# One of three weight sums of a seven-product pair moved from VectorE to an accumulating DMA

## The chip, the cores and the metric

The kernel runs on one core of a Trainium2 chip. A core has TensorE (PE: matmuls; PEld is its weight load, which overlaps them), VectorE (DVE), ScalarE (ACT), GpSimd (POOL) and SyncE (SP). Each of the five works through its own queue in order; semaphores order them against each other. SP, ACT and POOL can issue DMAs, which run on the core's 16 DMA engines. The metric is the device time of one execution in microseconds, as the median of several runs. The profile is one more execution, taken by the hardware profiler.

## The reference

A decoder trunk of two layers on 256 tokens of width 2048, in float32, beside 256 memory tokens. Only the matrix products matter here:

```python
mem_n = _rmsnorm(mem, norm_mem)
for layer in range(DEPTH):                                   # 2: HGRN2, then GLA
    hn = _rmsnorm(h, norm_mix[layer])
    y, xq = mixer(hn, w_in)                                  # gated linear recurrence on one input projection
    xa = _memory_attention(xq, mem_n, w_mem_kv[layer])
    h = h + jnp.concatenate([y, xa], axis=-1) @ w_out[layer]
    hn = _rmsnorm(h, norm_ffn[layer])
    gate, up = jnp.split(hn @ w_gate_up[layer], 2, axis=-1)  # 2048 -> 2 x 5632
    h = h + (jax.nn.silu(gate) * up) @ w_down[layer]         # 5632 -> 2048
return _rmsnorm(h, norm_final)
```

Every weight is read from HBM once, some 430 MB in all, and the 256 tokens make two tiles of 128.

## The kernel before, in words

**Products in parts.** A float32 operand is split in two parts of the narrower type `float32r`: the high part is a cast on ACT, the low part is what the cast left over, a subtraction on DVE (`split`, lines 276 to 291). A product of two operands is then three matmuls: high by high, high by low, low by high. Each has 128 rows and up to 512 columns.

**Pairs.** Weights come in tiles `raw` of 128 partitions by 4 blocks of 512 columns (1 MB, three buffers). Such a tile holds a *pair*: two row blocks (k = 0, 1) of the weight by two column blocks that begin at `c0` and `c1`. Against the two token tiles that is a 2 x 2 by 2 x 2 block product, which would take eight products. A pair of kind "S" takes seven, in the way of Strassen and Winograd, with sums of blocks on both sides (`seven`, lines 420 to 434): four blocks of a side and three sums that build on each other give seven factors. Kinds "O", "H" and "-" take eight products with fewer sums or none. An S pair costs 21 matmuls instead of 24. In return DVE has the sums of the weights to make, and seven blocks to split instead of four.

**An S pair's work before the change**, in the order in which DVE takes it: split of block 0 (one block, "a"), split of blocks 2 and 3 ("b"), then three sum instructions, in place in `raw` (one of two blocks at once, two of one block), then the splits of the sums, blocks 0 and 1 ("c") and blocks 2 and 3 ("d"). Each split is preceded by its cast on ACT. When "d" is done, the buffer is free, and SP can issue the loads of the pair three further on (`load_pair`, lines 408 to 418: two DMAs of 512 KB, first both row blocks of `c0`, then both of `c1`; the load's tile and the pair's parts wait for each other by semaphores that the framework sets). The split parts lie in six buffers `parts`, so DVE can run about two pairs ahead of PE.

**Sums on the other side.** The activations' factors are made once for each pair by `Forms.put` (feed-forward), `further` (mixers, output, memory), with the same three sums, on small tiles of 128 x 128.

**Where S pairs stand.** `project_two` (memory keys and values, mixers' input projections, the output projection, the last down projections) takes pairs by a plan such as "----SSS-". `project_halves` runs the gate/up projection: for each of 11 blocks of 512 columns eight pairs by a string of `KINDS`, "SSOSSOSS" for the last seven blocks of a layer; between two such blocks stand two down projections of an earlier part, with plain splits and no sums (`weights`, 4 tiles a block).

**What sets the order.** In the feed-forward, PE, DVE and ACT keep the program's order (`Engine.kept`); elsewhere the framework's scheduler orders each engine's queue by the program's order and readiness. Side work (decays, scores, readouts, transposes of the mixers) is cut in pieces and put between pairs (`later`, `step`). POOL does little: powers for the norms (`rstd`, line 189), memsets such as that of the scores `sc` (line 912), and one low part in each feed-forward block, which waits for a sum on DVE (`free_port`, line 286). No DMA is issued by POOL before the change.

Most operations are recorded at line 151, the wrapper that issues them; they are told apart by tiles: `raw<-raw` are the sums of weights, `parts<-raw` the splits, `f_p` the gate/up products, `fd` the down products, `hf`, `hv` those of HGRN, `gk`, `gg` of GLA, `wo` of the output, `m0p`, `m1p` of the memory.

Of the kernel before, what the change touches and what calls it, by code (L numbers as in the profile page):

```python
# [9 lines left out]
F32 = mybir.dt.float32  # L10
# [3 lines left out]
AF = mybir.ActivationFunctionType  # L14
ALU = mybir.AluOpType
AX = mybir.AxisListType

P = 128
# [22 lines left out]
def trunk_kernel(ctx: ExitStack, tc: tile.TileContext, x, mem, norm_mix, norm_ffn, norm_mem,  # L41
                 norm_final, hgrn_w_in, hgrn_lb_logits, hgrn_onorm, gla_w_in, gla_w_gk,
                 gla_b_gk, gla_onorm, w_mem_kv, w_out, w_gate_up, w_down, c_ident, c_mask, out):
    nc = tc.nc
# [117 lines left out]
    pe, ve, ac = Engine(nc.tensor), Engine(nc.vector), Engine(nc.scalar)  # L162
# [110 lines left out]
        n_w[0] += 1  # L273
        return i, wts.tile([P, 4, 512], F32, tag="raw", name=f"raw{i}", bufs=3)

    def split(src, name, by=2):

        n, m = src.shape[1:]
        if n == 1:
            both = wts.tile([P, 2, 1, 512], F32R, tag="part", name=f"parts{name}", bufs=2)  # L280
        else:
            both = wts.tile([P, 2, 2, 512], F32R, tag="parts", name=f"parts{name}", bufs=6)
        for k in range(0, n, by):
            j = min(k + by, n)
            ac.copy(out=both[:, 0, k:j, 0:m], in_=src[:, k:j, :])
            low = (nc.gpsimd if free_port else ve).tensor_tensor(  # L286
                out=both[:, 1, k:j, 0:m], in0=src[:, k:j, :], in1=both[:, 0, k:j, 0:m].bitcast(F32), op=ALU.subtract)
            if free_port:
                tc.add_manual_dep(low.ins, free_port.pop(), mybir.DependencyInfo(
                    mybir.DependencyClass.Sync, mybir.DependencyReason.DATA), reason="port")  # L290
        return [(both[:, 0, k, 0:m], both[:, 1, k, 0:m]) for k in range(n)]
# [67 lines left out]
    class Forms:  # L359
# [20 lines left out]
        def put(self, ps, gains):  # L380

            g = work.tile([P, 8, P], F32, tag="stg", name=f"{self.name}g", bufs=2)
            for k in range(2):
                ac.activation(out=g[:, 2 * k:2 * k + 2, :], in_=ps[:, 2 * k * P:(2 * k + 2) * P].rearrange(
                    "p (a t) -> p a t", t=P), func=AF.Copy, scale=gains[k])
            tt = ve.tensor_tensor

            def parts(i, j, n):
                ac.copy(out=self.h[:, i:i + n, :], in_=g[:, j:j + n, :])
                tt(out=self.l[:, i:i + n, :], in0=g[:, j:j + n, :], in1=self.h[:, i:i + n, :].bitcast(F32), op=ALU.subtract)  # L390

            if self.kind == "O":
                tt(out=g[:, 4:6, :], in0=g[:, 1:3, :], in1=g[:, 0:4:3, :], op=ALU.subtract)
                parts(0, 0, 6)
                return
            ve.scalar_tensor_tensor(out=g[:, 4, :], in0=g[:, 0, :], scalar=-1.0, in1=g[:, 3, :],
                                           op0=ALU.mult, op1=ALU.subtract)
            tt(out=g[:, 5, :], in0=g[:, 1, :], in1=g[:, 0, :], op=ALU.subtract)
            tt(out=g[:, 6, :], in0=g[:, 3, :], in1=g[:, 5, :], op=ALU.subtract)
            tt(out=g[:, 7, :], in0=g[:, 2, :], in1=g[:, 6, :], op=ALU.subtract)  # L400
            parts(0, 0, 8)
            if self.kind == "B":
                tt(out=g[:, 4, :], in0=g[:, 2, :], in1=g[:, 3, :], op=ALU.subtract)
                parts(8, 4, 1)

    TIMES = {"S": (1,) * 7, "O": (0, 2, 2, 2, 2, 0, 0), "H": (0, 2, 2, 2, 1, 0, 1)}

    def load_pair(raw, w, p, c0, c1, n):

        if n_w[0] == 1:  # L410
            for k, j, c in ((0, 0, c0), (0, 1, c1), (1, 3, c0), (1, 2, c1)):
                nc.sync.dma_start(out=raw[:, j, 0:n], in_=w[(2 * p + k) * P:(2 * p + k + 1) * P, c:c + n])
                if k == 0 and c == c1:
                    load_mem(0, 256, 512)
            return
        for j, c in ((slice(0, 4, 3), c0), (slice(1, 3), c1)):
            nc.sync.dma_start(out=raw[:, j, 0:n],
                              in_=w[2 * p * P:(2 * p + 2) * P, c:c + n].rearrange("(k p) c -> p k c", p=P))

    def seven(i, raw, between=None):  # L420

        n = raw.shape[2]
        tt = ve.tensor_tensor
        b00, = split(raw[:, 0:1, :], f"{i}a")
        b11, b10 = split(raw[:, 2:4, :], f"{i}b")
        if between:
            between()

        tt(out=raw[:, 0:2, :], in0=raw[:, 0:4:2, :], in1=raw[:, 1:2, :].broadcast_to([P, 2, n]), op=ALU.subtract)
        tt(out=raw[:, 2, :], in0=raw[:, 2, :], in1=raw[:, 0, :], op=ALU.add)  # L430
        tt(out=raw[:, 3, :], in0=raw[:, 3, :], in1=raw[:, 2, :], op=ALU.subtract)
        t5, t7 = split(raw[:, 0:2, :], f"{i}c")
        t6, t4 = split(raw[:, 2:4, :], f"{i}d")
        return {1: ("x00", b00), 2: ("x01", b10), 3: ("z", b11), 4: ("x11", t4), 5: ("s", t5), 6: ("u", t6), 7: ("d0", t7)}

    def further(g):

        tt = ve.tensor_tensor
        ve.scalar_tensor_tensor(out=g[:, 4, :], in0=g[:, 1, :], scalar=-1.0, in1=g[:, 3, :], op0=ALU.mult, op1=ALU.subtract)
        tt(out=g[:, 5, :], in0=g[:, 0, :], in1=g[:, 1, :], op=ALU.subtract)  # L440
        tt(out=g[:, 6, :], in0=g[:, 3, :], in1=g[:, 5, :], op=ALU.subtract)
        tt(out=g[:, 7, :], in0=g[:, 2, :], in1=g[:, 6, :], op=ALU.subtract)

    class Pair:

# [70 lines left out]
    def project_two(pairs, plan, w, c0, c1, n, name, give, view=lambda ps: ps, onto=None, prep=None, behind=None,  # L516
# [7 lines left out]
        ps, out = {}, []  # L524
# [35 lines left out]
        for at, (p, kind) in enumerate(zip(order, plan)):  # L560
            i, raw = new_raw()
            if i == 0:
                load_pair(raw, w, p, c0, c1, n)
            if prep:
                prep(at)
            if i > 0:
                load_pair(raw, w, p, c0, c1, n)
            if kind == "S":
                todo = held(behind, seven, i, raw[:, :, 0:n]) if behind else seven(i, raw[:, :, 0:n])
                last = at == plan.rindex("S")  # L570
                for b in (1, 6, 7, 5, 2, 4, 3) if last else (3, 2, 1, 5, 7, 6, 4):
                    product(b, pairs[p].get(todo[b][0]), todo[b][1])
                if last and at == len(plan) - 1:
                    early()
                elif len(pending) > MANY:
                    step()
                continue
            b00, b01 = split(raw[:, 0:2, 0:n], f"{i}a", 2 if i else 1)
            b11, b10 = split(raw[:, 2:4, 0:n], f"{i}b")
            if at > 0 and at == plan.rindex("S") + 1:  # L580
                early()
            for k, (lf, rt) in enumerate(((b00, b01), (b10, b11))):
                step()
                for b, t, right_factor in ((2, 0, lf), (4, 1, lf), (8, 1, rt), (3, 0, rt)):
                    if b == 8 and len(pending) > MANY:
                        step()
                    product(b, pairs[p].x(k, t), right_factor)
# [3 lines left out]
    def project_halves(forms, kinds, w, c0, c1, name, key, keep):  # L591
# [15 lines left out]
        for p, kind in enumerate(kinds):  # L607
            Engine.kept = keep <= p
            i, raw = new_raw()
            load_pair(raw, w, p, c0, c1, 512)  # L610
            x = forms[p].get
            last = p == len(PAIRS) - 1
            if kind == "S":
                todo = seven(i, raw, lambda: mark(key + p))
                for b in (1, 2, 6, 7, 5, 4, 3) if last else (1, 3, 2, 5, 7, 6, 4):
                    product(b, x(todo[b][0]), todo[b][1])
            else:
                b00, b01 = split(raw[:, 0:2, :], f"{i}a")
                mark(key + p)
                b11, b10 = split(raw[:, 2:4, :], f"{i}b")  # L620
                todo = [[(2, "x00", b00), (5, "x10", b01), (4, "x10", b00), (3, "d0", b01)]]
                if kind == "O":
                    todo.append([(2, "x01", b10), (5, "x11", b11), (4, "x11", b10), (3, "d1", b11)])
                else:
                    ve.tensor_tensor(out=raw[:, 3, :], in0=raw[:, 3, :], in1=raw[:, 2, :], op=ALU.subtract)
                    e1, = split(raw[:, 3:4, :], f"{i}c")
                    todo.append([(2, "x01", b10), (3, "x01", b11), (7, "x11", b11), (4, "x11", e1)])
                todo = [m for ms in zip(*todo) for m in ms] if last else todo[0] + todo[1]
                for b, f, right in todo:
                    product(b, x(f), right)  # L630
            step()
# [639 lines left out]
    scale = lambda ss=ss: h_scale(ss, "rx", True)  # L1271
    for l in range(2):
# [6 lines left out]
        turned = []  # L1279
# [26 lines left out]
        if l == 0:  # L1306
            hq = {}
            ffn(0, hq2, r2, lambda n: h_quad(hq, n, g_mix[1], ss, "hm1_", sevens=2))
            scale = lambda ss=ss: h_scale(ss, "rm1", True)
# [79 lines left out]
```

## Time and profile before

| | before |
|---|---|
| median of 3 runs | 2270.07 us (2270.04 to 2271.07) |
| the profiled execution's own time | 2271.69 us |
| its span | 2269.9 us |
| PE busy | 2250.8 us, 99% |
| DVE busy | 2065.8 us, 91% |
| ACT busy | 1423.5 us, 63% |
| POOL busy | 83.4 us, 4% |
| granted TensorE clock | 0.999 |
| read from HBM | 430.71 MB |

How to read it: busy time is the union of an engine's instructions. A group of instructions is written as line, engine, operation, out<-in, shapes, count, then busy us and mean ns of one, then the engine's idle time just before them and what ended it. The row of a wait names who waited, for whom, and the total, number and longest of the waits. In the chain, each piece has its start, its length and what it was. Windows count from the span's start.

### The profile page before, as it was taken

Reading aid. Unit: us, or ns where it says so; the run is one execution under the profiler, and the core shown is the slowest. Engines: PE = TensorE matmul, PEld = TensorE weight load, DVE = VectorE, ACT = ScalarE, POOL = GpSimd, SP = SyncE. Lnnn points to the kernel's source line nnn. Section 1 sums busy time; section 2 is a strip of 40 time slices with the busy share of each in tenths; the row PEclk is TensorE's granted clock in tenths of the full one; section 3 lists DMA queues with packets and bytes.
Section 4 is the critical chain, followed back from the end, with each engine's and each line's share of the span. In section 5 each row is a group of like instructions: output and inputs, shape, how many; then the busy total and the mean of one; then the engine's idle time right before and its main releaser. Section 6 shows DMA issues by size and latency. Waiting matters only on the chain.

```text
span 2269.9 us, 29374 instructions
## 1 busy us (share of the span) xinstructions
PE 2250.8 (99%) x10710; PEld 1901.4 (84%) x10710; DVE 2065.8 (91%) x2615; ACT 1423.5 (63%) x1938; POOL 83.4 (4%) x61
## 2 busy tenths in 40 slices
PE   9999999999999999999999999999999999999998
PEld 7888888888888888888889999988888888888887
DVE  7889999899999999999996887899899999999997
ACT  6655656566666666666665665566566666666664
POOL 0000000000000000000000000001000000000000
PEclk9999999999999999999999999999999999999999
DMA  8645545455556665555665446555556565665564
GB/s 289 204 151 183 186 157 177 167 168 203 170 202 222 204 206 190 203 199 204 204 212 174 142 146 190 157 176 203 197 194 203 205 210 194 205 205 202 205 217 153
DMA packets 232644, 435.78 MB, mean 192 GB/s; under 512 B 13199, under 2 KB 42675, under 8 KB 232243
## 3 DMA queue, kind: packets, MB, share of 16 engines
q1 hardware_dynamic: 231203, 429.64, 56.4%
q10 hardware_dynamic: 1296, 4.26, 0.5%
q8 instruction: 84, 1.38, 0.2%
q14 instruction: 61, 0.50, 0.1%
HBM read 430.71 MB, written 3.15 MB: 191 GB/s over the span
## 4 chain that ended last, share of the span: by engine, by line
PE 89%; DVE 6%; ACT 2%; issue 1%; DMA 1%; POOL 0%; SPq 0%; POOLq 0%; DVEq 0%; ACTq 0%
PE f_p L151 39%; PE fd L151 19%; PE wo L151 4%; PE m1p L151 2%; PE wo0p L151 2%; PE hf0p L151 2%; PE wo1p L151 2%; PE fd_0p L151 2%; PE gk1p L151 1%; PE gg11p L151 1%; PE gg10p L151 1%; PE gg01p L151 1%; PE m0p L151 1%; DVE raw L151 1%; PE gx L151 1%
## 5 line engine op out<-in xcount | busy, mean ns | idle before, releaser
L151 DVE TENSOR_TENSOR raw<-raw 128x512 f32<-128x512 f32 (+3 forms) x474 | 403.6, 852 | 9.2
L151 ACT CAST parts<-raw 128x1024 fp32r<-128x1024 f32 (+1 forms) x216 | 212.0, 1016 | 44.6 <-DMA raw<-in_w_down_dram 9.8
L151 DVE TENSOR_TENSOR parts<-raw,parts 128x1024 fp32r<-128x1024 f32 (+1 forms) x196 | 224.0, 1180 | 15.2 <-ACT parts L151 15.1
L286 POOL TENSOR_TENSOR parts<-raw,parts 128x1024 fp32r<-128x1024 f32 x20 | 48.2, 2411 | 1187.1 <-ACT parts L151 1138.6
L151 ACT COPY h<-fd 128x512 f32<-128x512 f32 x80 | 46.3, 588 | 55.0 <-PE fd L151 52.1
L151 ACT ACTIVATE s<-s,rf_r 128x512 f32<-128x512 f32 x44 | 31.8, 722 | 41.6 <-DVE s L151 41.4
L151 DVE TENSOR_TENSOR e<-f_p,e 128x512 f32<-128x512 f32 x66 | 45.2, 685 | 2.3
L151 ACT COPY fd<-h 128x512 f32<-128x512 f32 x82 | 45.2, 582 | 0.0
L151 PE MATMUL fd<-parts,s_6h 128*128 128x512 f32 x128 | 39.8, 392 | 0.0
L151 PE MATMUL fd<-parts,s_8h 128*128 128x512 f32 x128 | 39.8, 392 | 0.0
L151 PE MATMUL fd<-parts,s_4h 128*128 128x512 f32 x128 | 39.8, 392 | 0.0
L151 PE MATMUL fd<-parts,s_2h 128*128 128x512 f32 x128 | 39.8, 392 | 0.0
L151 PE MATMUL fd<-parts,s_0h 128*128 128x512 f32 x128 | 39.8, 392 | 0.0
L151 PE MATMUL fd<-parts,s_5h 128*128 128x512 f32 x128 | 39.4, 389 | 0.0
L151 PE MATMUL fd<-parts,s_3h 128*128 128x512 f32 x128 | 39.4, 389 | 0.0
L151 PE MATMUL fd<-parts,s_7h 128*128 128x512 f32 x128 | 39.4, 389 | 0.0
L151 PE MATMUL fd<-parts,s_1h 128*128 128x512 f32 x128 | 39.4, 389 | 0.0
L151 DVE TENSOR_TENSOR s<-f_p,e 128x512 f32<-128x512 f32 x44 | 30.3, 689 | 4.3 <-PE f_p L151 2.4
L151 DVE SCALAR_TENSOR_TENSOR s<-e,rf_r,s 128x512 f32<-128x512 f32 x44 | 31.0, 747 | 0.2
L151 PEld LDWEIGHTS fd<-parts,s_7h 128*128 128x128 f32 x128 | 24.0, 188 | 5.0
L151 PEld LDWEIGHTS fd<-parts,s_3h 128*128 128x128 f32 x128 | 24.0, 188 | 5.0
L151 PEld LDWEIGHTS fd<-parts,s_1h 128*128 128x128 f32 x128 | 24.0, 188 | 5.0
(5723 smaller groups left out, 7258.1 us busy)
## 6 DMA issues: line engine op xcount, KB each, us to landing
raw<-in_w_gate_up_dram SPq DMA_DIRECT2D x352, 512.0 KB, 3.9
raw<-in_w_down_dram SPq DMA_DIRECT2D x80, 1024.0 KB, 5.7
raw<-in_hgrn_w_in_dram SPq DMA_DIRECT2D x96, 512.0 KB, 3.9
raw<-in_gla_w_in_dram SPq DMA_DIRECT2D x96, 384.0 KB, 3.3
raw<-in_w_out_dram SPq DMA_DIRECT2D x16, 1024.0 KB, 5.8
raw<-in_w_out_dram SPq DMA_DIRECT2D x32, 512.0 KB, 4.1
raw<-in_w_mem_kv_dram SPq DMA_DIRECT2D x30, 512.0 KB, 5.5
raw<-in_w_down_dram SPq DMA_DIRECT2D x16, 512.0 KB, 4.1
```

The costliest lines, as they stand in the source:

```text
L151: ins = func(*args, **kwargs)
L286: low = (nc.gpsimd if free_port else ve).tensor_tensor(out=both[:, 1, k:j, 0:m], in0=src[:, k:j, :], in1=both[:, 0, k:j, 0:m].bitcast(F32) ...
```

## The change

Signs of the seven products are chosen anew, so that the first weight sum is a plain sum of two blocks as they lie in HBM, block 1 (k = 0, `c1`) plus block 2 (k = 1, `c1`). `load_pair` loads the `c1` half first, and for an S pair POOL then issues a DMA of 256 KB that adds block 2 from HBM onto block 1 in `raw`. It has to wait for the `c1` load, and the first sum on DVE has to wait for it. DVE keeps two sums: one of one block, which uses the added block, and one of two blocks. The split of blocks 0 and 1 is taken with the opposite sign (`turned`): ACT casts with scale -1, DVE makes the low part with a scalar_tensor_tensor. Before, that split gave the factors of products 5 and 7, now of 6 and 7, and the order of products follows. The sums of the activations change sign accordingly; in `Forms.put` two of them become one instruction.

```diff
-    def split(src, name, by=2):
+    def split(src, name, by=2, turned=False):
...
+            if turned:
+                hi = both[:, 0, k:j, 0:m]
+                ac.activation(out=hi, in_=src[:, k:j, :], func=AF.Copy, scale=-1.0)
+                ve.scalar_tensor_tensor(out=both[:, 1, k:j, 0:m], in0=src[:, k:j, :], scalar=-1.0, in1=hi.bitcast(F32),
+                                        op0=ALU.mult, op1=ALU.subtract)
+                continue
...
# Forms.put
-            ve.scalar_tensor_tensor(out=g[:, 4, :], in0=g[:, 0, :], scalar=-1.0, in1=g[:, 3, :],
-                                           op0=ALU.mult, op1=ALU.subtract)
-            tt(out=g[:, 5, :], in0=g[:, 1, :], in1=g[:, 0, :], op=ALU.subtract)
-            tt(out=g[:, 6, :], in0=g[:, 3, :], in1=g[:, 5, :], op=ALU.subtract)
-            tt(out=g[:, 7, :], in0=g[:, 2, :], in1=g[:, 6, :], op=ALU.subtract)
+            tt(out=g[:, 4:6, :], in0=g[:, 3:0:-2, :], in1=g[:, 0:1, :].broadcast_to([P, 2, P]), op=ALU.subtract)
+            ve.scalar_tensor_tensor(out=g[:, 6, :], in0=g[:, 3, :], scalar=-1.0, in1=g[:, 5, :],
+                                    op0=ALU.mult, op1=ALU.subtract)
+            tt(out=g[:, 7, :], in0=g[:, 2, :], in1=g[:, 6, :], op=ALU.add)
...
-    def load_pair(raw, w, p, c0, c1, n):
+    def load_pair(raw, w, p, c0, c1, n, kind):
...
-        for j, c in ((slice(0, 4, 3), c0), (slice(1, 3), c1)):
+        for j, c in ((slice(1, 3), c1), (slice(0, 4, 3), c0)):
             nc.sync.dma_start(out=raw[:, j, 0:n],
                               in_=w[2 * p * P:(2 * p + 2) * P, c:c + n].rearrange("(k p) c -> p k c", p=P))
+        if kind == "S":
+            nc.gpsimd.dma_start(out=raw[:, 1, 0:n], in_=w[(2 * p + 1) * P:(2 * p + 2) * P, c1:c1 + n], accum_op=ALU.add)
...
# seven
-        tt(out=raw[:, 0:2, :], in0=raw[:, 0:4:2, :], in1=raw[:, 1:2, :].broadcast_to([P, 2, n]), op=ALU.subtract)
-        tt(out=raw[:, 2, :], in0=raw[:, 2, :], in1=raw[:, 0, :], op=ALU.add)
-        tt(out=raw[:, 3, :], in0=raw[:, 3, :], in1=raw[:, 2, :], op=ALU.subtract)
-        t5, t7 = split(raw[:, 0:2, :], f"{i}c")
-        t6, t4 = split(raw[:, 2:4, :], f"{i}d")
+        tt(out=raw[:, 0, :], in0=raw[:, 1, :], in1=raw[:, 0, :], op=ALU.subtract)
+        tt(out=raw[:, 2:4, :], in0=raw[:, 2:4, :], in1=raw[:, 0:1, :].broadcast_to([P, 2, n]), op=ALU.subtract)
+        t6, t7 = split(raw[:, 0:2, :], f"{i}c", turned=True)
+        t5, t4 = split(raw[:, 2:4, :], f"{i}d")
...
# project_two, and the like in project_halves
-                for b in (1, 6, 7, 5, 2, 4, 3) if last else (3, 2, 1, 5, 7, 6, 4):
+                for b in (1, 6, 7, 5, 2, 4, 3) if last else (3, 2, 1, 6, 7, 5, 4):
```

More of the change, by code (lines that the diff above doesn't have):

```diff
@@ L438, in further @@
         tt = ve.tensor_tensor
-        ve.scalar_tensor_tensor(out=g[:, 4, :], in0=g[:, 1, :], scalar=-1.0, in1=g[:, 3, :], op0=ALU.mult, op1=ALU.subtract)
+        tt(out=g[:, 4, :], in0=g[:, 3, :], in1=g[:, 1, :], op=ALU.subtract)
         tt(out=g[:, 5, :], in0=g[:, 0, :], in1=g[:, 1, :], op=ALU.subtract)
-        tt(out=g[:, 6, :], in0=g[:, 3, :], in1=g[:, 5, :], op=ALU.subtract)
-        tt(out=g[:, 7, :], in0=g[:, 2, :], in1=g[:, 6, :], op=ALU.subtract)
+        ve.scalar_tensor_tensor(out=g[:, 6, :], in0=g[:, 3, :], scalar=-1.0, in1=g[:, 5, :], op0=ALU.mult, op1=ALU.subtract)
+        tt(out=g[:, 7, :], in0=g[:, 2, :], in1=g[:, 6, :], op=ALU.add)
     class Pair:
@@ L562, in project_two @@
             if i == 0:
-                load_pair(raw, w, p, c0, c1, n)
+                load_pair(raw, w, p, c0, c1, n, kind)
             if prep:
@@ L566, in project_two @@
             if i > 0:
-                load_pair(raw, w, p, c0, c1, n)
+                load_pair(raw, w, p, c0, c1, n, kind)
             if kind == "S":
@@ L609, in project_halves @@
             i, raw = new_raw()
-            load_pair(raw, w, p, c0, c1, 512)
+            load_pair(raw, w, p, c0, c1, 512, kind)
             x = forms[p].get
@@ L614, in project_halves @@
                 todo = seven(i, raw, lambda: mark(key + p))
-                for b in (1, 2, 6, 7, 5, 4, 3) if last else (1, 3, 2, 5, 7, 6, 4):
+                for b in (1, 2, 6, 7, 5, 4, 3) if last else (1, 3, 2, 6, 7, 5, 4):
                     product(b, x(todo[b][0]), todo[b][1])
```

## The prediction

> **What bounds the kernel now.** I read the page's busy times first, then the chain that ended last, then busy time by stage, then what TensorE (PE) waited for.
>
> ```profile
> span 2269.9 us, 29374 instructions
> PE 2250.8 (99%) x10710; PEld 1901.4 (84%) x10710; DVE 2065.8 (91%) x2615; ACT 1423.5 (63%) x1938; POOL 83.4 (4%) x61
> ```
>
> PE is covered for 99% of the span. A busy PE need not be a PE at its peak, so the chain, cut to one feed-forward block, gives the pace:
>
> ```profile
> 838.36 16.32 PE fd L151 x72
> 854.69 0.87 PE tp_s_5h L151 x8
> 855.56 5.46 PE fd L151 x24
> 861.02 39.65 PE f_p L151 x174
> ```
>
> 24 matmuls in 5.46 us are 227 ns each, 72 in 16.32 us the same, and 174 in 39.65 us are 228. Gate/up matmuls, fed by the sums that the change touches, run as fast as down matmuls, which have none. There is nothing to win inside such a block: one block costs 39.65 + 16.32 + 0.87 + 5.46 = 62.3 us of matmuls whatever VectorE (DVE) does. By stage (columns: busy us of PE, PEld, DVE, ACT, POOL, with counts; clock; DMA share; GB/s):
>
> ```profile
> 155.00:417.00 262.00, 257.22 (x1271) 214.03 (x1270) 250.23 (x346) 155.99 (x215) 6.82 (x7) 1.00 0.51 168
> 620.00:1180.00 560.00, 560.00 (x2502) 462.75 (x2501) 532.88 (x583) 360.75 (x443) 21.71 (x9) 1.00 0.60 203
> 798.72:861.02 62.30, 62.30 (x279) 51.44 (x279) 59.37 (x65) 40.10 (x49) 2.42 (x1) 1.00 0.60 203
> ```
>
> In the feed-forward (620 to 1180) PE never stops. In HGRN (155 to 417) it stands 4.8 us. DVE is nearly as full as PE: 59.37 of 62.30 us in one block, 2.9 us idle. What PE waited for (us in total, times, longest):
>
> ```profile
> PE spg L151 <- DVE GQ L151: 1.5, 1, 1.5
> PE hv0p L151 <- ACT parts34d L151: 0.9, 1, 0.9
> PE slh L151 <- DVE Th L151: 0.9, 2, 0.5
> PE hv2p L151 <- DVE y_1l L151: 0.7, 1, 0.7
> PE hv1p L151 <- ACT parts50d L151: 0.7, 1, 0.7
> PE gg00p L151 <- DVE parts238d L151: 0.5, 1, 0.5
> PE hv2p L151 <- DVE parts65d L151: 0.5, 1, 0.5
> PE hf2p L151 <- DVE parts58d L151: 0.5, 1, 0.5
> PE hf1p L151 <- DVE parts42d L151: 0.4, 1, 0.4
> PE m0p L151 <- DVE parts6d L151: 0.3, 1, 0.3
> PE gg00p L151 <- ACT parts238d L151: 0.2, 1, 0.2
> PE f_p L151 <- DVE parts359d L151: 0.2, 1, 0.2
> ```
>
> The waits for a "d" part, the last split of a seven-product pair and so the end of its chain of sums, add up to 0.9 + 0.7 + 0.5 + 0.5 + 0.5 + 0.4 + 0.3 + 0.2 + 0.2 = 4.2 us. That is what a shorter chain can win at most; the three other DVE waits (1.5 + 0.9 + 0.7 = 3.1 us) lie on other DVE work and move only as DVE is freer.
>
> **The change part by part.** The groups of instructions that it touches (mean ns of one after the busy us):
>
> ```profile
> L151 DVE TENSOR_TENSOR raw<-raw 128x1024 f32<-128x1024 f32 x144 | 175.7, 1220 | 0.3
> L151 DVE TENSOR_TENSOR raw<-raw 128x768 f32<-128x768 f32 x10 | 9.6, 955 | 0.2
> L151 DVE TENSOR_TENSOR raw<-raw 128x512 f32<-128x512 f32 x300 | 207.5, 692 | 8.4
> L151 DVE TENSOR_TENSOR parts<-raw,parts 128x1024 fp32r<-128x1024 f32 x180 | 212.7, 1222 | 3.7 <-ACT parts L151 3.7
> L151 DVE SCALAR_TENSOR_TENSOR s<-e,rf_r,s 128x512 f32<-128x512 f32 x44 | 31.0, 747 | 0.2
> L151 ACT CAST parts<-raw 128x1024 fp32r<-128x1024 f32 x200 | 201.8, 1047 | 33.0 <-DMA raw<-in_w_down_dram 9.8 <-DMA raw<-in_w_out_dram 7.9 <-PE m1p L151 5.4
> L151 ACT ACTIVATE ab<-ab 128x1024 f32<-128x1024 f32 x4 | 4.2, 1061 | 0.1
> ```
>
> Each seven-product pair has one double-width sum, so there are 144 + 10 = 154 of them.
>
> *Sums.* Before: 1220 + 2 x 692 = 2604 ns; after: 692 + 1220 = 1912. Saved: 0.69 us a pair.
>
> *The turned split.* Its DVE half becomes a scalar_tensor_tensor. At 512 columns that form costs 747 against 692; at 1024 I bound its extra cost between 0 and 0.11 us. Its ACT half goes from 1047 to about 1061 ns. Before, that cast lay under 1.38 us of the other two sums; now it lies under one sum of 1.22 us, which still covers it. So DVE keeps 0.5 to 0.69 us a pair; I take 0.6, 154 x 0.6 = 92 us of its 2065.8. In a full block with six such pairs DVE's idle time grows from 2.9 to 2.9 + 3.6 = 6.5 us. PE gets none of that, as 62.3 us are matmuls.
>
> *Factors and product order.* One small DVE operation fewer in each Forms; the products fed by the turned split go first, in the order in which the splits end. Both lie under running matmuls: 0. Without that cover a Forms is worth 0.3 us.
>
> *SP.* The two loads of a pair swap. They are issued 0.4 us apart (two in 0.88 us, in a row below), so c0 lands 0.4 us later, and ACT's first cast needs it. Where the cast waits for a load anyway, an S pair starts 0.4 us later; DVE's saving of 0.6 us on the same pair covers it. Cost 0.
>
> *The accumulating DMA.* 128 x 512 x 4 bytes are 0.262 MB, 128 x 384 x 4 are 0.197: 144 x 0.262 + 10 x 0.197 = 39.7 MB more. POOL issues it, having waited for the c1 load to land; the DVE sum waits for its own landing. No row shows one. The nearest:
>
> ```profile
> q1 hardware_dynamic: 231203, 429.64, 56.4%
> raw<-in_w_gate_up_dram SPq DMA_DIRECT2D x352, 512.0 KB, 3.9
> raw<-in_w_mem_kv_dram SPq DMA_DIRECT2D x4, 256.0 KB, 5.9
> maskf<-in_mask_dram SPq DMA_DIRECT2D x1, 256.0 KB, 2.8
> L189 POOL TENSOR_TENSOR ro_r<-ro_v,mhalf 128x4 f32<-128x4 f32 x6 | 6.0, 1006 | 92.6 <-DVE ro_v L151 92.6
> ```
>
> At q1's price (56.4% for 429.64 MB) it takes 5.2% of the DMA engines, at twice that for reading and writing back 10%; at a share of 0.60 there is room. Its latency, from landing of the load to landing of the sum: at least the quiet 256 KB load, 2.8 us; at most the crowded one plus one POOL operation, 5.9 + 1.0 = 6.9 us. I take 3.9 + 1.0 = 4.9 us: a load in the same traffic plus POOL's part. How long may it take? The rows of two S pairs, the SP issues and then the first sum:
>
> ```profile
> 741.01 0.88 SPq L417 DMA_DIRECT2D raw<-in_w_gate_up_dram  x2
> 751.66 1.22 DVE L151 TENSOR_TENSOR raw<-raw 128x1024 f32<-128x1024 f32 x1
> 234.85 1.25 SPq L417 DMA_DIRECT2D raw<-in_hgrn_w_in_dram  x2
> 242.88 1.23 DVE L151 TENSOR_TENSOR raw<-raw 128x1024 f32<-128x1024 f32 x1
> ```
>
> In the block, c1 lands at 741.0 + 3.9 = 744.9, and the sum starts at 751.7, or 751.1 with an S pair ahead that is 0.6 us shorter: 6.2 us of room. In HGRN, with the same 3.9, 234.85 + 3.9 = 238.75 to 242.88: 4.1 us. So 4.9 us is hidden in the block, and 0.8 us late at the first S pair of an HGRN group, where three S pairs then save 1.8 us; their "d" waits (0.4 and 0.5) still go. Behind the waiting sum on DVE stand all its later splits; behind the waiting DMA on POOL stand the r factors and memsets of the mixers.
>
> The Trainium skill, "DMA: Bandwidth & Descriptors", section "Anatomy of one DMA — SWDGE (gpsimd) path", puts a transfer issued from POOL at about 2.0 us plus its bytes over 436 GB/s; as an estimate that is 2.6 us here, and by it nothing would be late even in HGRN, with the sum the same 4.2 us.
>
> *Sum.* PE loses the 4.2 us of "d" waits and gains none: 2270.07 - 4.2 = 2265.9, say 2266.0. The profiled execution took 2271.69 (span 2269.9 and 1.8 around it), 1.6 above the median that I subtract from; a profile of after should show a span near 2265.7.
>
> **The rivals.**
>
> *The DMA is late enough to become the bound (slower).* In a full block (SSOSSOSS) I give the room of 6.2 us to four of the six S pairs, the other two having an S pair and longer work ahead; DVE can lose 6.5 us in all, 1.6 us each. So the point from which it decides is 6.2 + 1.6 = 7.8 us of latency. Each us above costs 4 us in each of the 14 blocks with six S pairs, 56 us. At 9 us: 14 x 4 x 1.2 = 67 us, 2337. For it: no transfer here was issued by POOL, POOL takes 2411 ns for a form and shape that DVE does in 1222, and DVE, which it may have to wait for, is 95% busy (532.88 of 560):
>
> ```profile
> L286 POOL TENSOR_TENSOR parts<-raw,parts 128x1024 fp32r<-128x1024 f32 x20 | 48.2, 2411 | 1187.1 <-ACT parts L151 1138.6 <-DVE s L151 48.5
> L151 DVE TENSOR_SCALAR K<-F 128x1024 f32<-128x1024 f32 x3 | 2.1, 695 | 0.1
> ```
>
> Against it: 6.9 us was the worst bound. The Trainium skill, "SBUF — State Buffer", section "Who interferes with whom", says that POOL cannot write the descriptors of its transfers while DVE runs copy, cast or tensor_scalar in a two-port mode, and that tensor_tensor has no such mode. The trace agrees as to the modes: tensor_scalar took 695 ns for 1024 columns, tensor_tensor 1220; the former is rare in a block, so by that page the latency stays short, and the lock itself no run shows yet.
>
> *POOL's order (slower, mild).* POOL takes its work in order. The memset of the scores waits long for PE or DVE ("sch", here), and an accumulating DMA put behind it waits as well:
>
> ```profile
> L912 POOL MEMSET sch<- 128x1024 f32 x3 | 2.9, 956 | 224.3 <-PE po L151 96.1 <-DVE ro_v L151 95.4 <-PE ao L151 32.9
> ```
>
> Five such memsets (three here, two more in GLA by the code); the wait can eat the room of 4 to 6 us before it costs, and I estimate 1 to 3 us of PE each, about the one 2.8 us load: +5 to +15, less 4.2 won, about 2276. Against it: POOL is busy 4% of the span, so most places in its queue harm nothing; which one is drawn this trace can't tell.
>
> *Nothing comes of it.* The "d" waits are replaced by waits for the accumulated sum at the same places, or another schedule outside the feed-forward shifts as much as is won: 2270, give or take 2.
>
> *More comes of it.* With DVE freer the other three waits shrink too: 4.2 + 3.1 = 7.3, 2262.8.
>
> **How the numbers follow.** 0.2% of the time, 4.5 us, is about what a measurement of this kernel can tell from no change. The forecast, a gain of 2 to 6.5 us (2263.5 to 2268), has 0.48, half on either side of 4.5 us. More comes of it: 0.08, faster. Nothing: 0.18, same. POOL's order: 0.13, of which 0.03 same. The late DMA: 0.13, slower. Faster 0.24 + 0.08 = 0.32; same 0.24 + 0.18 + 0.03 = 0.45; slower 0.10 + 0.13 = 0.23. The range goes from just below the larger gain, 2261.5, up through POOL's order, 2281; it leaves out the late DMA and a little below.
>
> **What would show it.** Right: DVE busy near 1974; 154 fewer raw sums of 128x512; f_p still 228 ns a matmul; landing of POOL's DMA near 4.9 us; the "d" rows gone from PE's waits. Wrong: rows "DVE raw <- DMA raw" of more than 1 us each in the feed-forward, PE under 560 of 560 us there, or accumulating DMAs that POOL issues long after their load landed.

## The result, and the profile after

| | before | after |
|---|---|---|
| median | 2270.73 us (2269.32 to 2274.14, 20 runs) | 2275.19 us (2270.77 to 2277.97, 20 runs) |
| ratio after / before | | 1.0017 [1.0010, 1.0024] |
| profiled execution, span | 2271.69, 2269.9 us | 2272.82, 2271.0 us |

The change made the kernel some 4 us slower; 2266.0 was forecast. The page of after, busy times, queues, POOL's issues:

```profile
span 2271.0 us, 30130 instructions
PE 2247.5 (99%) x10710; PEld 1904.3 (84%) x10710; DVE 1974.3 (87%) x2449; ACT 1429.7 (63%) x1938; POOL 210.9 (9%) x215
...
q1 hardware_dynamic: 231203, 429.64, 56.1%
q0 software_dynamic: 22176, 39.72, 11.1%
...
L425 POOL DMA_DIRECT2D raw<-in_w_gate_up_dram x114 | 98.9, 867 | 990.2 <-DMA raw<-in_w_gate_up_dram 670.1
...
raw<-in_w_gate_up_dram POOLq DMA_DIRECT2D x114, 256.0 KB, 5.4
```

DVE lost 91.5 us of work (2065.8 to 1974.3). The sums of weights of after, by shape:

```profile
L151 DVE TENSOR_TENSOR raw<-raw 128x1024 f32<-128x1024 f32 x144 | 176.4, 1225 | 4.1
L151 DVE TENSOR_TENSOR raw<-raw 128x512 f32<-128x512 f32 x156 | 107.5, 689 | 44.1 <-DMA raw<-in_w_gate_up_dram 34.0 <-DMA raw<-in_hgrn_w_in_dram 3.2 <-DMA raw<-in_w_mem_kv_dram 2.6
L151 DVE TENSOR_TENSOR raw<-raw 128x384 f32<-128x384 f32 x10 | 5.6, 557 | 14.2 <-DMA raw<-in_gla_w_in_dram 10.1 <-issue 3.2 <-DVE parts237a L151 0.5
```

The last column is DVE's idle time just before these sums. It stood 34.0 us for POOL's DMAs in the gate/up blocks and 10.1 us in GLA.

Where the time went, by two landmarks in each trace: the first product of the first gate/up block that is a group of its own (`parts85a`) and the first output product of layer 1 (`parts276a`). The two numbers ahead of the semicolon are the first and last start. Before:

```profile
L151 PE MATMUL f_p<-parts85a,hf_1h x8: 387/394/476, 529.3 to 531.7; 128*128 128x512 f32 x8
L151 PE MATMUL wo1p<-parts276a,y_2h x8: 389/389/389, 1505.8 to 1508.1; 128*128 128x512 f32 x8
```

After:

```profile
L151 PE MATMUL f_p<-parts85a,hf_1h x8: 387/394/476, 521.8 to 524.2; 128*128 128x512 f32 x8
L151 PE MATMUL wo1p<-parts276a,y_2h x8: 389/389/389, 1508.1 to 1510.4; 128*128 128x512 f32 x8
```

At the start of the feed-forward after is 529.3 - 521.8 = 7.5 us ahead, more than was forecast for the whole kernel. At the end of GLA it is 2.3 us behind. The windows place both, HGRN (250 to 400) and GLA (1250 to 1500). Before:

```profile
250.00:400.00 150.00, 146.69 (x735) 121.69 (x734) 141.56 (x204) 91.42 (x138) 5.86 (x6) 1.00 0.51 169
1250.00:1500.00 250.00, 247.65 (x1446) 238.49 (x1445) 204.42 (x336) 154.96 (x243) 6.93 (x14) 1.00 0.53 168
```

After, with the feed-forward between them:

```profile
250.00:400.00 150.00, 149.98 (x754) 126.13 (x753) 141.06 (x202) 92.99 (x138) 12.92 (x14) 1.00 0.61 186
620.00:1180.00 560.00, 560.00 (x2509) 464.64 (x2508) 504.09 (x535) 363.54 (x443) 65.84 (x60) 1.00 0.75 229
1250.00:1500.00 250.00, 238.96 (x1382) 229.17 (x1382) 190.68 (x303) 145.61 (x220) 15.91 (x24) 0.99 0.57 170
```

In HGRN PE stands 0.0 us instead of 3.3. In GLA it stands 11.0 instead of 2.4. The longest waits of PE after:

```profile
PE slg L151 <- DVE GQ L151: 3.5, 2, 2.3
PE slg L151 <- ACT GQ L151: 2.4, 1, 2.4
PE tgk L151 <- ACT gsk L151: 1.8, 2, 1.0
PE zp L151 <- DVE gk L151: 1.8, 1, 1.8
```

No row for a "d" part is left; the new ones are GLA's own small work (`GQ`, `gk`). DVE's queue in GLA tells why. After, with idle time and its end in brackets:

```profile
1414.55 0.56 DVE L151 TENSOR_TENSOR parts262a<-raw,parts262a 128x384 fp32r<-128x384 f32 x1 [0.39 <-ACT parts262a L151]
1418.13 0.56 DVE L151 TENSOR_TENSOR raw<-raw 128x384 f32<-128x384 f32 x1 [3.02 <-DMA raw<-in_gla_w_in_dram]
1418.61 0.95 DVE L151 TENSOR_TENSOR parts261b<-raw,parts261b 128x768 fp32r<-128x768 f32 x1
1419.47 1.28 DVE L151 COPY_PREDICATED scg<-mask,spg 128x128 f32<-128x128 uint8 x4
1420.55 0.73 DVE L151 TENSOR_TENSOR GK<-GK,Tg 128x512 f32<-128x512 f32 x1
1421.19 0.68 DVE L151 TENSOR_TENSOR GQ<-GQ,Tg 128x512 f32<-128x512 f32 x1
```

The DMA that this sum needs, in the timeline of POOL, was issued only at 1413.56. The buffer of pair 262 had come free when the split `parts259b`, of the pair three earlier, ended at 1408.84, and load and added block run one after the other from there:

```profile
1413.56 0.86 POOL L425 DMA_DIRECT2D raw<-in_gla_w_in_dram  x1 [5.68 <-DVE GQ L151]
```

And in PE's timeline the product `slg` stopped 2.39 us for a `GQ` that ACT copies at 1421.39 from `GK`, and that `GK` stands behind the sum in DVE's queue:

```profile
1417.42 2.25 PE L151 MATMUL gg10p<-parts259a,hm_5x 128*128 128x384 f32 x12
1422.06 1.16 PE L151 MATMUL slg<-GQ 128*128 128x128 f32 x8 [2.39 <-ACT GQ L151]
```

The first sum of pair 262 was put right behind its "a" split, ahead of the previous pair's "b" split and six operations of the recurrence (four masks, `GK`, `GQ`). DVE works in order, so for 3.02 us all of them stood behind a transfer, though they needed nothing of it. Before, at the same place, the sum needed only what was there:

```profile
1417.10 0.55 DVE L151 TENSOR_TENSOR parts262a<-raw,parts262a 128x384 fp32r<-128x384 f32 x1
1417.68 0.96 DVE L151 TENSOR_TENSOR raw<-raw 128x768 f32<-128x768 f32 x1
1418.56 0.44 DVE L151 COPY_PREDICATED scg<-mask,spg 128x128 f32<-128x128 uint8 x1
1418.79 0.99 DVE L151 TENSOR_TENSOR parts261b<-raw,parts261b 128x768 fp32r<-128x768 f32 x1
```

### The profile page after: what moved, and what is told of

It is laid out like the page before. It is cut to its first block, busy times and chain, and to the rows that moved or that the text cites. A ratio compares the mean times of both kernels' runs of the same rounds, so it can differ in the third digit from the quotient of the medians.

```text
span 2271.0 us, 30130 instructions
## 1 busy us (share of the span) xinstructions
PE 2247.5 (99%) x10710; PEld 1904.3 (84%) x10710; DVE 1974.3 (87%) x2449; ACT 1429.7 (63%) x1938; POOL 210.9 (9%) x215
## 3 DMA queue, kind: packets, MB, share of 16 engines
q1 hardware_dynamic: 231203, 429.64, 56.1%
q0 software_dynamic: 22176, 39.72, 11.1%
## 4 chain that ended last, share of the span: by engine, by line
PE 94%; DVE 2%; DMA 2%; issue 1%; ACT 0%; SPq 0%; POOL 0%; POOLq 0%; DVEq 0%; ACTq 0%
PE f_p L151 39%; PE fd L151 19%; PE wo L151 4%; PE m1p L151 2%; PE hv2p L151 2%; PE hv1p L151 2%; PE hv0p L151 2%; PE wo0p L151 2%; PE wo1p L151 2%; PE hf2p L151 2%; PE hf1p L151 2%; PE fd_0p L151 2%; PE m0p L151 2%; PE gg01p L151 1%; PE hf0p L151 1%; DMA raw<-in_gla_w_in_dram 1%
## 5 line engine op out<-in xcount | busy, mean ns | idle before, releaser
L151 DVE TENSOR_TENSOR raw<-raw 128x512 f32<-128x512 f32 (+3 forms) x320 | 299.0, 934 | 62.7 <-DMA raw<-in_w_gate_up_dram 34.0
L425 POOL DMA_DIRECT2D raw<-in_w_gate_up_dram x114 | 98.9, 867 | 990.2 <-DMA raw<-in_w_gate_up_dram 670.1
L151 DVE TENSOR_TENSOR s<-f_p,e 128x512 f32<-128x512 f32 x44 | 30.3, 690 | 10.1 <-PE f_p L151 8.2
L425 POOL DMA_DIRECT2D raw<-in_hgrn_w_in_dram x17 | 14.8, 872 | 216.0 <-DMA raw<-in_hgrn_w_in_dram 125.9
```

The costliest lines, as they stand in the source:

```text
L151: ins = func(*args, **kwargs)
L425: nc.gpsimd.dma_start(out=raw[:, 1, 0:n], in_=w[(2 * p + 1) * P:(2 * p + 2) * P, c1:c1 + n], accum_op=ALU.add)
```

## The experiments

Medians of one group of runs stand beside the kernel before on the same chip: 2270.37 us for the first four, 2270.49 for the next four, 2269.87 for the last three. Two questions: what GLA lost, and where HGRN's gain came from.

**The changed kernel again**, unedited.

> The changed kernel itself once more, for a second profile beside the others of this call. Theory A (VectorE, which works in order, blocks in GLA on accumulating DMAs that the scheduler took to be early, with the score work behind it): time 2273 to 2277, TensorE again some 9 us ahead of before at the end of the first layer, and GLA some 10 us longer than before, with VectorE waiting for those DMAs about 10 us there. Theory B (the extra DMA traffic as such costs time everywhere, by a varying amount): the loss stands elsewhere in this profile than in the first one, in the feed-forward stages too.

2274.21 us, ratio 1.0017 [1.0008, 1.0026]. A second profile came out at 2276.0 us, 5 us above the first. DVE's wait for GLA's DMAs had grown in it (window 1235 to 1500; us in total, times, longest), from 10.1 in 3 to:

```profile
DVE raw L151 <- DMA raw<-in_gla_w_in_dram: 12.2, 4, 4.4
```

**GLA's ten sums back on DVE.** Only the ten pairs of 384 columns lose the accumulating DMA.

```diff
# load_pair
-        if kind == "S":
+        if kind == "S" and n == 512:
# seven, ahead of the first sum
+        if n < 512:
+            tt(out=raw[:, 1, :], in0=raw[:, 1, :], in1=raw[:, 2, :], op=ALU.add)
```

> No accumulating DMA in GLA (10 of 154 pairs, those 384 columns wide): there VectorE adds the two blocks itself, with the new signs. Theory A: GLA takes its old length, so about 10 us less than the changed kernel, 2263 to 2266, faster than before by 0.2 to 0.3%. Theory B: 10 of 154 transfers are 6% of the traffic, so within 1 us of the changed kernel, 2274 to 2276.

2262.98 us, ratio 0.9969 [0.9956, 0.9981]. That is theory A's time, and theory B falls: ten transfers fewer were worth 2274.2 - 2263.0 = 11.2 us.

**All DMAs stay, GLA's first sum is held.** In GLA the first sum is ordered on DVE behind its own pair's "b" split, so that it cannot be put ahead of it (`hold` names the instruction behind which the next one is ordered).

```diff
# seven, ahead of the first sum
+        if n < 512:
+            ve.hold = ve.last
         tt(out=raw[:, 0, :], in0=raw[:, 1, :], in1=raw[:, 0, :], op=ALU.subtract)
```

> All 154 accumulating DMAs stay; in GLA alone the first sum is ordered behind the pair's second split on VectorE, so it is asked for later. Theory A: the waits for the DMA in GLA go from about 10 us to under 2, time 2263 to 2268, like the kernel without DMAs in GLA. Theory B: same traffic, so the same time as the changed kernel, 2274 to 2276. A third theory C (POOL's transfers in GLA disturb VectorE or POOL's own work there, whoever waits): 2272 to 2276, with few waits for the DMA but GLA still long.

2262.77 us, ratio 0.9964 [0.9951, 0.9976]. GLA's window of the held kernel:

```profile
1250.00:1500.00 250.00, 247.75 (x1433) 237.23 (x1432) 202.08 (x328) 154.25 (x235) 17.72 (x26) 1.00 0.59 180
```

PE is busy 247.75 us there, as before the change (247.65), with every accumulating DMA in place. A window cuts off a part of a stage that got longer, so the whole of GLA is measured better from its first product on `parts224a` to the first output product. The starts of both, before and after (`wo1p` is shown above):

```profile
L151 PE MATMUL gk0p<-parts224a,hm_1x x12: 334/334/423, 1242.4 to 1244.8; 128*128 128x384 f32 x12
L151 PE MATMUL gk0p<-parts224a,hm_1x x12: 334/334/423, 1233.4 to 1235.8; 128*128 128x384 f32 x12
```

In the held kernel:

```profile
L151 PE MATMUL gk0p<-parts224a,hm_1x x12: 334/334/422, 1232.8 to 1235.2; 128*128 128x384 f32 x12
L151 PE MATMUL wo1p<-parts276a,y_2h x8: 389/389/389, 1495.9 to 1498.2; 128*128 128x512 f32 x8
```

GLA took 1505.8 - 1242.4 = 263.4 us before, 1508.1 - 1233.4 = 274.7 after, and 1495.9 - 1232.8 = 263.1 in the held kernel. So GLA lost some 11 us (2274.2 - 2262.8 = 11.4 by the medians) by the place of ten sums in DVE's order, and not by traffic, POOL, or a lack of time on DVE.

**No accumulating DMA at all.** Signs, load order and turned split stay new, DVE makes all three sums.

```diff
# load_pair
-        if kind == "S":
+        if False:
# seven, ahead of the first sum
+        tt(out=raw[:, 1, :], in0=raw[:, 1, :], in1=raw[:, 2, :], op=ALU.add)
```

> No accumulating DMA at all: VectorE makes the third sum in all 154 pairs, but signs, load order, the turned split and the order of products are those of the changed kernel. Theory A: the waits for the last split of a pair in HGRN come back, GLA is as before: 2269 to 2273, VectorE busy about 2070 us. A fourth theory D (the new order of loads or products, or the new schedule that goes with the signs, lengthens GLA): GLA is still some 10 us longer than before and HGRN has its old waits, 2277 to 2281.

2264.88 us, ratio 0.9975 [0.9966, 0.9984]: 5.5 us faster than before, with none of the DMAs. That was no theory's forecast. With the held order the DMAs add only 2264.9 - 2262.8 = 2.1 us to it. So something else in the diff brings most of the gain. A candidate stood in PE's record of the last pair of a block. Before, product 6 takes "d" ahead of "c":

```profile
896.67 0.39 PE L151 MATMUL f_p<-parts155b,hf_7l 128*128 128x512 f32 x1
896.89 0.78 PE L151 MATMUL f_p<-parts155d,hf_7h 128*128 128x512 f32 x2
```

After, in the same place, product 6 takes "c":

```profile
888.75 0.39 PE L151 MATMUL f_p<-parts155b,hf_7l 128*128 128x512 f32 x1
888.98 0.62 PE L151 MATMUL f_p<-parts155c,hf_7h 128*128 128x512 f32 x2
```

Two such matmuls take 0.62 us where nothing holds them and took 0.78 before. The order of products in the last S pair of a group (1, 6, 7, 5, ... and 1, 2, 6, 7, 5, ...) is not in the diff. But the signs moved product 6 from the split "d", the end of the chain of sums, to "c", which is ready earlier.

**The kernel before, with 6 and 5 swapped in last pairs.** Nothing of the change.

```diff
-                for b in (1, 6, 7, 5, 2, 4, 3) if last else (3, 2, 1, 5, 7, 6, 4):
+                for b in (1, 5, 7, 6, 2, 4, 3) if last else (3, 2, 1, 5, 7, 6, 4):
...
-                for b in (1, 2, 6, 7, 5, 4, 3) if last else (1, 3, 2, 5, 7, 6, 4):
+                for b in (1, 2, 5, 7, 6, 4, 3) if last else (1, 3, 2, 5, 7, 6, 4):
```

> The kernel before, with nothing of the change, but in the last S pair of a group products 6 and 5 change places in the order of products, so that the two products that the split 'c' feeds (5 and 7 with the old signs) come before the one that 'd' feeds (6). With the new signs the unchanged order (1, 6, 7, 5, ...) has 6 and 7 from 'c', so the change made this swap by the way. Theory F (the gain outside GLA is the swap: the PE waits for 'd' were all in last pairs, where 'd' was asked for first): 2264 to 2267, like the kernel with new signs and no accumulating DMA (2264.9); the 'd' waits gone from PE's waits, a full block 62.1 us instead of 62.3. Rival G (the gain came from the order of the loads, c1 first, or from another schedule through the new signs): 2269 to 2272, 'd' waits still there.

2264.80 us, ratio 0.9977 [0.9968, 0.9985]. A block's gate/up products, in its chain, took 39.65 us before; here:

```profile
857.52 39.44 PE f_p L151 x174
```

Its waits for last splits:

```profile
PE hv0p L151 <- DVE parts34c L151: 0.7, 1, 0.7
...
PE gg00p L151 <- DVE parts238d L151: 0.5, 1, 0.5
...
PE hv1p L151 <- DVE parts50c L151: 0.5, 1, 0.5
PE gg00p L151 <- ACT parts238d L151: 0.4, 1, 0.4
```

Two lines of product order give 5.7 us. At the landmark `parts85a` this kernel is 3.1 us ahead of before (526.2 against 529.3), and 0.21 us in each of the 14 blocks with six S pairs are, by estimate, 2.9 more. HGRN's waits for "d" became shorter ones for "c" (0.7 + 0.5 us); GLA's stay, so the forecast that all of them go was too much.

**No accumulating DMA, and "d" asked for first again.** The same two new orders of last pairs, in the kernel without the DMA; with the new signs they bring "d" (product 5) ahead of "c".

> The kernel after without the accumulating DMA (DVE makes all three sums, signs and load order new), and in last pairs product 5 ahead of 6, so that with the new signs 'd' is again asked for ahead of 'c', as before the change. Theory F: the gain of 5.5 us of the kernel without this edit goes again: 2269 to 2272, 'd' waits back, a full block 62.3 us. Rival G (loads, signs): 2264 to 2266.

2267.89 us, ratio 0.9990 [0.9981, 0.9999]. Waits for "d" come back, smaller than before the change:

```profile
PE hv1p L151 <- ACT parts50d L151: 0.5, 1, 0.5
...
PE hv0p L151 <- ACT parts34d L151: 0.4, 1, 0.4
...
PE hv0p L151 <- DVE parts34d L151: 0.3, 1, 0.3
```

And the block's chain is slow again:

```profile
858.29 39.64 PE f_p L151 x174
```

So with the new signs the order is worth some 3 us (2.6 us under the kernel before, against 5.5); theory F, which had all 5.5 go again, is half right. The 2.6 us that are left lie in the load order, the turned split or the schedule that they lead to; these were not taken apart.

**All DMAs, GLA held, "d" asked for first.** What the DMA wins by itself.

> The kernel after with all accumulating DMAs, the first sum in GLA held behind the split 'b' (2262.8 without a further edit), and in last pairs product 5 ahead of 6, so that 'd' is asked for first as before the change. This measures what the accumulating DMA alone wins. As predicted (the DMA takes 0.6 us a pair off DVE, so that the 'd' waits go whatever the order): 2262 to 2264, no 'd' waits. Theory F in its strong form (the DMA wins nothing here, 'd' waits stay): 2267 to 2270. Between the two: the DMA wins part of them.

2263.98 us, ratio 0.9977 [0.9966, 0.9987], 3.9 us under the same kernel without the DMA. Of HGRN's "d" waits one of 0.2 us is left, and the block's chain is at its fast pace:

```profile
854.86 39.44 PE f_p L151 x174
```

So a DVE with less to do also removes most of these waits, as I had argued, but not all, as the forecast had it: PE's "d" waits still add up to 1.9 us here, 1.1 of them new, at the last pair ahead of a down projection (`fd_0p` for `parts210d`). The two gains overlap. Against the kernel before in the same group of runs the gains are 2.6 us (neither), 5.5 (the order), 6.5 (the DMA) and 7.6 (both): the order adds 2.9 us without the DMA and 1.1 with it, the DMA 3.9 and 2.1. Of these small steps the medians alone are not proof, as neighbouring intervals overlap; the blocks' 39.64 and 39.44 and the waits that come and go show where they lie, not their exact size.

**What the freed time buys.** First, much: the third pair of the last seven gate/up blocks gets seven products.

```diff
# on the held kernel
-    PAIRS = "SSOSSOSB"
+    PAIRS = "SSSSSOSB"
-    KINDS = ("SHOSHOSO", "HHOSSOSO", "SHOSSOSO", "SSOSSOHS", "SSOSSOSS")
+    KINDS = ("SHHSHOSO", "HHHSSOSO", "SHHSSOSO", "SSHSSOHS", "SSSSSOSS")
```

> The held kernel (2262.8), and the time that DVE has won is spent: the third pair of the gate/up blocks, of eight products, becomes one of seven in the last seven blocks of each layer (of kind H, also eight products, in the first four). 3 matmuls of 227 ns fewer in 14 blocks: 9.5 us. DVE gets some 3.8 us more a block, 56.8 + 3.8 = 60.6 of 61.4 us. If the accumulated sums land in time: 2253 to 2256. If DVE becomes the bound because it waits for them (it waits some 34 us in 560 for them in the kernel after): 2260 or more.

2315.51 us, ratio 1.0202 [1.0186, 1.0217]. The feed-forward window:

```profile
620.00:1180.00 560.00, 544.63 (x2399) 442.84 (x2398) 510.69 (x536) 360.70 (x442) 70.95 (x66) 1.00 0.76 224
```

DVE's largest group of waits in it:

```profile
DVE raw L151 <- DMA raw<-in_w_gate_up_dram: 29.2, 15, 3.6
```

PE stands 15.4 us of 560 and starts 109 matmuls fewer than in the held kernel (2399 against 2508). DVE is busy no more than 510.69 us, but 29.2 us go to sums that were not there yet. In the held kernel the same window has 15.7 us of such waits, the longest 1.6, and PE is busy for all of it. That DVE has no slack left here to take longer waits is my reading of these numbers; no run with these pairs and without the DMAs tests it.

Then little: one H pair more becomes S in each of the first four blocks of a layer, which costs DVE about what the DMAs take off it there.

```diff
# on the held kernel
-    KINDS = ("SHOSHOSO", "HHOSSOSO", "SHOSSOSO", "SSOSSOHS", "SSOSSOSS")
+    KINDS = ("SSOSHOSO", "SHOSSOSO", "SSOSSOSO", "SSOSSOSS", "SSOSSOSS")
```

> The held kernel with the accumulating DMAs (2262.8), and one pair more of seven products in each of the first four gate/up blocks of a layer, where one of kind H (eight products) stood; the other blocks stay at six S pairs. 4 x 2 x 3 = 24 matmuls fewer, 24 x 0.227 = 5.4 us. Such a change costs DVE two block splits more, some 2.4 us, about what the accumulating DMAs take off it in such a block (4 x 0.6). If that is what the saving is worth: 2256 to 2259. If a sum that lands late takes it back, as in the kernel with seven S pairs a block (+3 us a block): 2262 or more.

2258.27 us, ratio 0.9947 [0.9935, 0.9960]: the fastest here, 11.6 us under the kernel before where the held kernel was 7.6 under it. 4.0 of 5.4 us came. Its first blocks:

```profile
516.00:790.00 274.00, 274.00 (x1234) 227.24 (x1233) 250.19 (x272) 178.18 (x223) 32.90 (x30) 1.00 0.75 224
```

The same in the third and fourth block alone:

> As the kernel with four more, but only in the third and fourth block, where DVE is busy 53.7 and 54.7 of 62 us; the fourth is then like the seven blocks behind it, which run at PE's pace with the DMA. 12 matmuls fewer, 2.7 us: 2259 to 2261.

2263.05 us, ratio 0.9963 [0.9949, 0.9976]. That misses its forecast of 2259 to 2261: it is 6.8 us under the kernel before, where the held kernel was 7.6 under it, so nothing of the 2.7 us came. Its profile shows two waits of PE for one late pair (323c, 1.6 + 0.8 us); whether they are in the other executions too isn't known.

And the four S pairs in the kernel before with swapped products, without any DMA:

> The kernel before with products 6 and 5 swapped in last pairs (2264.8, no accumulating DMA), and the same four more S pairs a layer, which cost DVE here 2.4 + 0.7 = 3.1 us each. If DVE's time is what the DMA buys, the 5.4 us aren't reached: 2262 to 2275. If they are reached without the DMA (2258 to 2261), DVE had room before and the accumulating DMA isn't what pays for them.

2270.21 us, ratio 1.0000 [0.9991, 1.0009]: the swap's 5.7 us are gone, by the same edit that wins 4.0 with the DMAs. Its first blocks, where PE stands 1.8 us and DVE is busy 264.97 instead of 250.19 us:

```profile
516.00:790.00 274.00, 272.20 (x1217) 223.73 (x1216) 264.97 (x299) 175.69 (x219) 10.70 (x5) 1.00 0.59 200
```

Without the four pairs the two kernels stood 7.6 - 5.7 = 1.9 us apart, with them 11.9. So what the accumulating DMA buys is room on DVE, and that is worth more when work that was refused for lack of it is put there. How much fits isn't said by that: seven S pairs a block were too many, and the two pairs alone won nothing.

## Why the prediction was wrong

*DVE's saving.* Right: 91.5 us measured, 92 forecast, 0.59 us a pair. In number 144 sums of 512 columns and ten of 384 went (300 to 156, 20 to 10), not 154 of 512.

*The "d" waits vanish.* They did: none is left, and at the start of the feed-forward PE was 7.5 us ahead, more than the 4.2 us. The reason given was half of it. The DMA alone wins 3.9 us, and the order alone 2.9 with the new signs and 5.7 with the old.

*"Factors and product order: 0".* This step failed. I looked at the order that the diff edits, (5, 7, 6, 4) to (6, 7, 5, 4), where nothing happens, and not at the order of last pairs that the diff leaves as it is while the signs change what it means. All the "d" waits that I quoted in HGRN, GLA and the feed-forward were in such last pairs; asking which product waited would have shown it.

*"One block costs 62.3 us of matmuls whatever DVE does".* Wrong by 0.2 us a block with six S pairs: f_p went from 39.65 to 39.44, 227 ns a matmul where 228 was to stay. The mean of 228 held a short stall, most of it at the first product of "d" (0.78 us for two matmuls against 0.62), which busy time does not show, since 560.00 of 560 us are busy in both. It shows in counts (2502 to 2509 matmuls).

*The latency of the DMA.* Forecast 4.9 us from the landing of the load, POOL's part included; from POOL's issue alone the median in the gate/up blocks is 5.4. That lies within the bounds of 2.8 to 6.9, but single transfers don't: the longest of the 154 took 9.1.

The rows "DVE raw <- DMA raw" in the feed-forward, which I named as a sign of trouble, came: 34.0 us in 42 waits, the longest 2.3. They cost PE nothing in this profile, where DVE's idle time had grown from 27.1 to 55.9 of the 560 us, about the 6.5 us a block that I gave it. In the second profile of the same kernel one sum came 4.7 us late, and PE waited 0.9 us for `parts383c` behind it: the late DMA, which I had as the large rival, exists as a single case. Whether POOL issues long after a load has landed, my third sign, the trace doesn't settle: 72 of the 114 issues in the gate/up blocks followed a DMA's landing, for the others it names something else.

The Trainium skill, "DMA: Bandwidth & Descriptors", section "Anatomy of one DMA — SWDGE (gpsimd) path", would by estimate give 2.6 us; the median here is twice that, in traffic, and the measurement decides. The rule cited from "SBUF — State Buffer" in the Trainium skill, that POOL writes no descriptors while DVE runs copy, cast or tensor_scalar in a two-port mode, isn't tested by any run here; an issue took POOL 867 ns in the mean.

*GLA.* This step failed too, and it turned the sign: the sum has no term for it ("PE loses the 4.2 us of "d" waits and gains none"). I examined the room of the DMA in a gate/up block, where the order is kept, and in HGRN, but not in GLA, whose DVE queue the scheduler orders among the recurrence's own operations. I wrote that all later splits stand behind a waiting sum; in GLA it was `GQ`, `GK` and the masks as well, and PE waits for them (3.5 and 2.4 us in the rows above). The cost was 11.4 us. A schedule outside the feed-forward that shifts as much as is won was one of the rivals, but only as a wash of 2 us either way, and POOL's order, the slower rival nearest in time, is not what happened: holding ten sums on DVE, with the same transfers left to POOL, brought all of it back. That the measured 2275.19 lies next to that rival's 2276 is chance.

The sum as measured: -5.5 for signs and order, -2.1 for the DMA on top, +11.4 for GLA's order, together +3.8. It meets 2274.21 - 2270.37 = 3.8 by construction, as its terms are differences of the same medians; the first comparison gave 2275.19 - 2270.73 = 4.5.

## What to carry to other kernels

When a step is handed to a transfer, look at every queue in which its consumer stands, and at who orders that queue: where a scheduler does, tie the consumer behind work that certainly ends later than the transfer. When the meaning of an index changes (here, which split feeds product 6), follow it through the lines that the diff does not touch. And time freed on an engine that is not the bound is worth little until it is spent, and what can be spent is found by trying: here one more S pair in each of the first four blocks of a layer won 4.0 us, and one more in each of the last seven (with an H pair in place of an O in the first four) lost some 50.

## What the runs showed of the hardware

The accumulating DMA took 11.1% of the DMA engines for 39.72 MB, 0.279% a MB, where the plain loads took 56.1% for 429.64 MB, 0.131% a MB: 2.1 times the price, just above the upper bound of 10% that I had set. 5.4 us at the median for 256 KB in the gate/up blocks is longer than the plain load of 512 KB beside it, 4.2 us in the same profile:

```profile
raw<-in_w_gate_up_dram SPq DMA_DIRECT2D x352, 512.0 KB, 4.2
```

That load itself took 3.9 us before. The accumulating DMA's median differs by stage in the profile after: 4.0 us at the output projection, 4.2 in HGRN, 7.1 at the four in the last down projections, and 3.7 in GLA for its 192 KB.
